# The first shift of the opening: half of its sum on VectorE for the latents, the context's part behind the first product

## Chip, core and metric

One NeuronCore of one Trainium2 chip runs the whole kernel. The metric is the device time of one execution in microseconds (us).

## The reference

One layer of a diffusion backbone over 1024 latent tokens with a prefix of 256 context tokens, width 1024, all in float32. Every sub-layer is normalised and then modulated by a shift, a scale and a gate, which are linear in SiLU of a conditioning vector: `c` for the latents, `c_ctx` for the context. The part that matters here, cut short:

```python
mod_lat = silu(c) @ w_mod + b_mod        # (1, 9 * 1024): nine pieces of 1024
mod_ctx = silu(c_ctx) @ w_mod + b_mod
ml, mc = split(mod_lat, 9), split(mod_ctx, 9)

def modulate(h, shift, scale):
    return h * (1.0 + scale) + shift

x  = x  + 0.5 * ml[2] * swiglu(modulate(rms_norm(x,  g1), ml[0], ml[1]), ffn1_w_in, ffn1_w_out)
cx = cx + 0.5 * mc[2] * swiglu(modulate(rms_norm(cx, g1), mc[0], mc[1]), ffn1_w_in, ffn1_w_out)
# then: short convolution and attention, merged; a second FFN; a final norm of x
```

So piece 0 of `w_mod` (1024 x 1024) gives the first shift, piece 1 the first scale, each for two vectors. The latents need them before the first matrix product of FFN 1 can start; the context needs them much later, since its tokens are read only after the latents' FFN is under way.

## The kernel before

Tokens lie along the free dimension, features along the 128 partitions. The latents come in two halves of 512 tokens, C0 and C1; the two-by-two blocks of each FFN product are formed by a Strassen-Winograd scheme with seven products (the class `Winograd`). A float32 operand is split into two parts (a rounded one and the rest), and each product is three matmuls: `split` takes a cast on ScalarE and a subtraction on VectorE or, where `lo_engines` says so, on GpSimd (POOL). Matrix tiles in the profile: `wl` and `wh` are split weights, `r` split left operands, `ps`, `pt`, `po` PSUM banks (five, two and one of them), `raw` a loaded weight, `rawm` a loaded tile of `w_mod`, `xtok` loaded tokens.

The program has one stretch at its beginning in which `strict[0]` is true: there every instruction of every engine, and every load in the queue of SyncE (SP), keeps the order in which the program writes it. After that a planner with costs of its own orders what is left free. The stretch in question, in the order written:

1. `fetch_tokens(C0)` loads four tiles of tokens, `fetch_mod(1, 0)` and `fetch_mod(0, 0)` load the first 512 columns of the scale and of the shift as four tiles of 512 KB each. Each tile holds two blocks of 128 rows of `w_mod`, so there are eight blocks, k = 0 to 7.
2. TensorE turns tokens. `mod10 = column_mod(1, 0, ...)` and `mod00 = column_mod(0, 0, ...)` make the first half of the scale and of the shift: for each k a matmul with the two columns of SiLU (latents and context) as the weights and the block (128 x 512) as the moving operand, all eight summed in one bank as two rows. The float32 product shows as two matmul records for each k. ScalarE copies the two rows (`mrow`), four small transposes turn them into columns, and `column_adds` on VectorE adds the bias into `modl` and `modc`. Both are generators; `run(g, n)` takes n steps of one.
3. `part_gain` makes the gain from the scale, and for each of four k `left_operand(0, k, mod11)` applies gain and shift to a tile of scaled tokens (VectorE for even k, ScalarE for odd) and splits it into `r`. Between the operands stand steps of `mod11 = second_mod(1, 1, ...)`: the other half of the scale for the latents alone, summed on VectorE in `macc` with one instruction for each k, the sum over the partitions by four matmuls against a column of ones (`summed_mod`). `part_gain` for the context stands behind the first operand.
4. `half1.start_together()` yields the first products of FFN 1 one by one: `run(start, 1)` first gives the two products for columns 0 and 1, each copied from its bank by ScalarE into `uc`, then one product a step. `half1.prefetch(n)` fills the list of loaded and split weights up to n.
5. Between these steps stand the rest of the opening: `scaled(k, pt)` (a copy of turned tokens by ScalarE, a scaling by VectorE), `turn` (the transposes of the tokens for the next two banks), the other half of the shift (`raws01`, `mod01`), the squares and transposes of the tokens of C1.

Of the kernel before, what the change touches and what calls it, by code (L numbers as in the profile page):

```python
# [9 lines left out]
F32 = mybir.dt.float32  # L10
# [3 lines left out]
ALU = mybir.AluOpType  # L14
# [4 lines left out]
P = 128  # L19
D = 1024  # L20
KD = D // P
# [28 lines left out]
def tile_dit_layer(  # L50
# [44 lines left out]
    act, dve, pool, pe, sp = (Engine(e) for e in (nc.scalar, nc.vector, nc.gpsimd, nc.tensor, nc.sync))  # L95

    const = ctx.enter_context(tc.tile_pool(name="const", bufs=1))
# [9 lines left out]
    def uniq(s):  # L107
        n_tiles[0] += 1
        return f"{s}_{n_tiles[0]}"
# [4 lines left out]
    def ttile(name, n=512, dt=F32):  # L114
        t = tpool.tile([P, 512], dt, tag="t", name=uniq(name))
        return t[:, :n]
# [4 lines left out]
    def ps_s(n=512):  # L121
        return psum.tile([P, 512], F32, tag="s", name=uniq("ps"), bufs=5)[:, :n]

    def ps_t(n=512):
        return psum.tile([P, 512], F32, tag="t", name=uniq("pt"), bufs=2)[:, :n]
# [4 lines left out]
    def matmul(out, w, x, start, stop, pinned=False, on=False):  # L130

        inst = pe.matmul(out, w, x, start=start, stop=stop, skip_group_check=on)
        if pinned:
            tc.keep_in_program_order(inst)

    def transpose(out, in_, pinned=False):
        n = in_.shape[0]
        inst = pe.transpose(out, in_, ident[:n, :n])
        if pinned:
            tc.keep_in_program_order(inst)  # L140
# [8 lines left out]
    make_identity(nc, ident[:])  # L149
    ones = const.tile([P, 1], F32, name="ones")  # L150
    dve.memset(ones[:], 1.0)
    ones_r = const.tile([P, 1], F32R, name="ones_r")
    act.copy(out=ones_r[:], in_=ones[:])

# [21 lines left out]
    def col(name, k=0):  # L176
        o = voff[name] + k
        return cols[:, o : o + 1]

    silu_c = const.tile([P, 16], F32, name="silu_c")  # L180
# [3 lines left out]
    modc = const.tile([P, 40], F32, name="modc")  # L184
# [113 lines left out]
    def summed_mod(m, half, acc):  # L298
        pm = ps_s(4)
        for j in range(4):  # L300
            matmul(pm[:, j : j + 1], acc[:, j * P : (j + 1) * P], ones[:], start=True, stop=True)
        column_adds(m, half, pm, (0,))

    def fetch_mod(m, half):
        raws = []
        for kk in range(KD // 2):
            raw = atile("rawm", (P, 2, 512))
            o = m * D + half * 512
            src = w_mod[0, kk * 256 : (kk + 1) * 256, o : o + 512].rearrange("(a p) n -> p a n", p=P)
            load(raw[:], src)  # L310
            raws.append(raw)
        return raws

    def column_adds(m, half, pm, streams):
        c0 = m * 8 + half * 4
        for i, v in enumerate(streams):
            dve.tensor_add(
                out=(modl, modc)[v][:, c0 : c0 + 4], in0=pm.rearrange("p (k v) -> p v k", v=len(streams))[:, i],
                in1=bcol[:, c0 : c0 + 4],
            )  # L320

    def column_mod(m, half, raws, bank):

        sc = silu_c[:].rearrange("p (v k) -> p k v", k=KD)
        pr = bank()
        for k in range(KD):
            matmul(pr[:2], sc[:, k], raws[k // 2][:, k % 2], start=(k == 0), stop=(k == KD - 1))
            if k % 2 and k < KD - 1:
                yield
        row = ttile("mrow")  # L330
        act.copy(out=row[:2], in_=pr[:2])
        yield
        pm = ps_t(8)
        for j in range(4):
            transpose(pm[:, 2 * j : 2 * j + 2], row[:2, j * P : (j + 1) * P])
        column_adds(m, half, pm, (0, 1))
        yield

    def second_mod(m, half, raws):

        acc = ttile("macc")
        for k in range(KD):
            raw, s = raws[k // 2][:, k % 2], silu_c[:, k : k + 1]
            if k:
                dve.scalar_tensor_tensor(out=acc, in0=raw, scalar=s, in1=acc, op0=ALU.mult, op1=ALU.add)
            else:
                dve.tensor_scalar(out=acc, in0=raw, scalar1=s, scalar2=None, op0=ALU.mult)
            yield
        yield
        summed_mod(m, half, acc)  # L350
        yield
        yield
# [9 lines left out]
    def part_gain(t, m, gname, s, a, b):  # L362
        mod, c0, o = (modl if s == "l" else modc), (m + 1) * 8, voff[gname]
        dve.tensor_scalar(
            out=t[:, a:b], in0=mod[:, c0 + a : c0 + b], scalar1=1.0, scalar2=math.sqrt(D), op0=ALU.add, op1=ALU.mult
        )
        dve.tensor_mul(out=t[:, a:b], in0=t[:, a:b], in1=cols[:, o + a : o + b])
# [70 lines left out]
    def run(steps, n=None):  # L438

        if n is None:  # L440
            for _ in steps:
                pass
        else:
            for _ in range(n):
                next(steps, None)
# [620 lines left out]
    def fetch_tokens(ch):  # L1066
        s, o, n = ch
        src = x[0] if s == "l" else ctxt[0]
        toks = []
        for j in range(n // P):  # L1070
            t = atile("xtok")
            load(t[:], src[o + j * P : o + (j + 1) * P, :])
            toks.append(t)
        return toks
# [17 lines left out]
    load_vectors("b", [("b", b_mod[0])])  # L1092
    t0 = fetch_tokens(C0)
    raws10, raws00 = fetch_mod(1, 0), fetch_mod(0, 0)
    mod10, mod00 = column_mod(1, 0, raws10, ps_t), column_mod(0, 0, raws00, ps_o)

    def column_pairs(w, offsets):
        return [tuple(w[:, o : o + P] for o in ab) for ab in offsets]
# [2 lines left out]
    gain1 = {s: const.tile([P, 8], F32, name=f"gain1_{s}") for s in "lc"}  # L1101
# [14 lines left out]
    def turn(toks, k, pt):  # L1116
        for j, t in enumerate(toks):
            transpose(pt[:, j * P : (j + 1) * P], t[:, k * P : (k + 1) * P])
# [10 lines left out]
    def left_operand(i, k, between=iter(())):  # L1129
        h, c = h0[k][:, i], k + 4 * i  # L1130
        if k % 2 == 0:
            dve.tensor_scalar(
                out=h, in0=h, scalar1=gain1["l"][:, c : c + 1], scalar2=modl[:, c : c + 1], op0=ALU.mult, op1=ALU.add
            )
        else:
            half1.shifted(h, c)
        run(between, 1 - k % 2)
        half1.keep(1 + i, k, h)
        run(between, 1 - k % 2)
# [6 lines left out]
    pr = ttile("pr")  # L1146
# [6 lines left out]
    run(mod10)  # L1153
    part_gain(gain1["l"], 0, "g1", "l", 0, 4)
    half1.prefetch(4, lo_engines=(pool, pool))
    run(mod00, 3)
    t1 = fetch_tokens(C1)
    raws11 = fetch_mod(1, 1)
    banks = {k: ps_s() for k in (4, 5)}
    for k, pt in banks.items():  # L1160
        turn(t0, k, pt)
    run(mod00)
    mod11 = second_mod(1, 1, raws11)
    for k in range(4):
        left_operand(0, k, mod11)
        if k == 0:
            part_gain(gain1["c"], 0, "g1", "c", 0, 4)
    start = half1.start_together()
    half1.prefetch(5, lo_engines=(pool, pool))
    for k, pt in banks.items():  # L1170
        scaled(k, pt)
    run(mod11, 2)
    run(start, 1)
    half1.prefetch(4, lo_engines=(pool, pool))
    banks = {k: ps_t() for k in (6, 7)}
    for k, pt in banks.items():
        turn(t0, k, pt)
        scaled(k, pt)
    raws01 = fetch_mod(0, 1)
    mod01 = second_mod(0, 1, raws01)  # L1180
    squares1 = token_squares(t1, ss1)
    run(mod11, 3)
# [120 lines left out]
    def context_rows(j):  # L1303

        raws = []
        for i in (j - 1, j):
            t = atile("raw")
            load(t[:], ffn1_w_out[0, i * P : (i + 1) * P, :])
            raws.append(t)
        return raws  # L1310
# [36 lines left out]
    for j in range(NH):  # L1347
        half1.side = side(j) if j >= SIDE_FROM else None
        if j > SIDE_FROM and j % 2:
            raws = context_rows(j)  # L1350
        u, c = half1.next_first()
        v, b = half1.second(u)
# [3 lines left out]
        if j == SIDE_FROM - 1:  # L1356
            for i in range(SIDE_FROM):
                if i % 2 == 0:
                    raws = context_rows(i + 1)
# [101 lines left out]
    for i in range(KD):  # L1461
# [6 lines left out]
        for ch, bg, gc in mixed():  # L1468
# [6 lines left out]
            for j in (0, 2):  # L1475
# [3 lines left out]
                    out=ya, in0=u[:, a + j - 1 : b + j - 1], scalar=col(f"w{j}", i), in1=ya, op0=ALU.mult, op1=ALU.add  # L1479
# [396 lines left out]
    for j in range(4):  # L1876
# [7 lines left out]
        out=gf[:], in0=cols[:, voff["gf"] : voff["gf"] + 8], scalar1=math.sqrt(D), scalar2=None, op0=ALU.mult  # L1884
# [96 lines left out]
    for j in range(NH):  # L1981
        if j > 1:
            run(late_steps, 3)
        u, c = fast.next_first()
        v, b = fast.second(u)
# [79 lines left out]
```

## Time and profile before

| | us |
|---|---|
| median of 3 runs (2669.16 to 2673.95) | 2670.07 |
| the profiled execution | 2671.16 |
| its span, first to last instruction | 2669.3 |
| TensorE matmuls, busy | 2628.8 |
| TensorE weight loads, busy | 2224.4 |
| VectorE busy | 2052.6 |
| ScalarE busy | 1192.0 |
| POOL busy | 548.8 |

The mean granted clock of TensorE was 0.996 of full speed. Rows of the timeline give the start, the duration, the engine, the line (nearly all have that of a helper, L88), the operation, the tile written and the tiles read, the shape, the count of merged instructions, and in brackets how long the engine was idle before and what ended that. PE is TensorE's matmul, PEld its weight load, DVE VectorE, ACT ScalarE, SPq the load queue of SyncE. In the table of stretches the columns are the stretch, its length, busy time and number of instructions for the engines, the granted clock, the busy share of the DMA engines and GB/s.

### The profile page before, as it was taken

The page shows a single profiled execution, that of the slowest core. Times are in us where ns is not written, and L with a number is a line of the kernel's source. Part 1 is how long each engine was busy: PE and PEld are TensorE (multiplying, and loading weights), DVE is VectorE, ACT ScalarE, POOL GpSimd, SP SyncE. Part 2 cuts the span into 40 slices and gives each one's busy share as a digit, 9 for nine tenths or more (in the row PEclk, how much of TensorE's full clock was granted, in tenths as well). Part 3 has the DMA queues.
Part 4 walks back from the last instruction along what each step waited for, and adds up shares of the span by engine and source line. Part 5 has one row for each costly group of instructions (what it writes and reads, how often), then busy time and mean ns, then how long its engine had stood idle before and what let it go on. Part 6 is the DMA issues. An engine that isn't in the chain of part 4 may idle for free. (4 is left out here: it accounts for less than half of the span.)

```text
span 2669.3 us, 37458 instructions
## 1 busy us (share of the span) xinstructions
PE 2628.8 (98%) x13557; PEld 2224.4 (83%) x13557; DVE 2052.6 (77%) x3412; ACT 1192.0 (45%) x2376; POOL 548.8 (21%) x425
## 2 busy tenths in 40 slices
PE   8999999999999999999999999999999999999998
PEld 5787998888888888888999888878788888888888
DVE  5988887875887899778687666786887787667975
ACT  5633443333454643333345666674346333334543
POOL 1244011211110044322033211000120444230200
PEclk9999999999999999999999999999999999999998
DMA  7655753335973444434413311003425654228731
GB/s 269 240 182 175 234 169 119 111 99 208 284 171 115 136 144 147 129 123 138 154 48 111 107 45 47 28 25 107 150 79 172 191 172 128 91 83 310 166 80 64
DMA packets 374769, 370.62 MB, mean 139 GB/s; under 512 B 28070, under 2 KB 264760, under 8 KB 374584
## 3 DMA queue, kind: packets, MB, share of 16 engines
q1 hardware_dynamic: 365560, 350.93, 39.9%
q0 software_dynamic: 9024, 17.30, 4.1%
q8 instruction: 106, 1.74, 0.3%
q14 instruction: 79, 0.65, 0.1%
HBM read 299.97 MB, written 68.16 MB: 138 GB/s over the span
## 5 line engine op out<-in xcount | busy, mean ns | idle before, releaser
L88 PE MATMUL ps<-r,wl 128*128 128x512 f32 x5496 | 1269.2, 391 | 15.5 <-DVE wl L88 7.7
L88 PEld LDWEIGHTS ps<-r,wl 128*128 128x128 f32 x5496 | 1028.2, 188 | 234.7 <-DVE wl L88 10.9
L88 ACT CAST wl<-s 128x512 fp32r<-128x512 f32 x266 | 164.1, 620 | 343.5 <-PE ps L88 259.1
L88 POOL TENSOR_TENSOR s<-raw 128x512 f32<-128x512 f32 x68 | 102.4, 1507 | 928.6 <-DMA raw<-in_ffn_w_in_dram 284.3
L88 ACT CAST wl<-raw 128x512 fp32r<-128x512 f32 x298 | 184.0, 620 | 206.4 <-PE ps L88 137.3
L88 DVE TENSOR_TENSOR wl<-raw,wl 128x512 fp32r<-128x512 f32 x296 | 209.4, 713 | 82.5 <-ACT wl L88 81.5
L88 DVE TENSOR_TENSOR wl<-s,wl 128x512 fp32r<-128x512 f32 x266 | 234.6, 883 | 29.9 <-ACT wl L88 28.3
L88 POOL TENSOR_TENSOR s<-raw,s 128x512 f32<-128x512 f32 x68 | 103.2, 1518 | 397.8 <-DVE wl L88 394.5
L88 DVE SCALAR_TENSOR_TENSOR macc<-rawm,silu_c,macc 128x512 f32<-128x512 f32 x168 | 146.4, 884 | 10.5 <-DMA rawm<-in_w_mod_dram 9.2
L88 PE MATMUL ps<-wh,r 128*128 128x256 f32 x768 | 142.2, 285 | 0.0
L88 DVE TENSOR_TENSOR u<-u,ps 128x512 f32<-128x512 f32 x171 | 116.1, 679 | 32.6 <-PE ps L88 31.9
L88 DVE TENSOR_TENSOR pts<-pt,pts 128x512 fp32r<-128x512 f32 x160 | 108.9, 687 | 39.3 <-ACT pts L88 38.0
L88 ACT CAST rh<-hid 128x512 fp32r<-128x512 f32 x132 | 81.5, 621 | 116.9 <-PE ps L88 100.4
L88 DVE TENSOR_REDUCE m<-ps 128x1 f32<-128x512 f32 (+1 forms) x192 | 111.0, 596 | 27.9 <-PE ps L88 27.0
L88 ACT CAST pts<-pt 128x512 fp32r<-128x512 f32 x160 | 93.0, 593 | 80.4 <-PE pt L88 80.0
L88 PE MATMUL ps<-rh,wl 128*128 128x512 f32 x360 | 122.1, 389 | 0.0
L88 PEld LDWEIGHTS ps<-wh,r 128*128 128x128 f32 x768 | 120.7, 192 | 0.2
L88 PE MATMUL po<-pts,vh 128*128 128x512 f32 x256 | 110.2, 437 | 0.8 <-ACT pts L88 0.7
L88 DVE TENSOR_TENSOR rl<-hid,rh 128x512 fp32r<-128x512 f32 x132 | 90.4, 687 | 26.7 <-ACT rh L88 12.3
L88 PE MATMUL ps<-wl,r 128*128 128x256 f32 x384 | 109.0, 284 | 0.0
L88 PE MATMUL ps<-kl,qs 128*128 128x512 f32 x384 | 105.9, 397 | 0.4 <-ACT pc L88 0.4
L88 POOL TENSOR_TENSOR s<-raw,raw 128x512 f32<-128x512 f32 x68 | 104.7, 1540 | 4.0 <-DVE macc L88 2.7
(300 smaller groups left out, 4892.7 us busy)
## 6 DMA issues: line engine op xcount, KB each, us to landing
raw<-in_ffn_w_in_dram SPq DMA_DIRECT2D x128, 512.0 KB
raw<-in_ffn_w_out_dram SPq DMA_DIRECT2D x72, 512.0 KB
rawm<-in_w_mod_dram SPq DMA_DIRECT2D x128, 256.0 KB
raw<-in_w_in_dram SPq DMA_DIRECT2D x61, 512.0 KB
hid<-hd SPq DMA_DIRECT2D x40, 512.0 KB
ws<-in_ffn_w_out_dram POOLq DMA_DIRECT2D x30, 512.0 KB, 6.5
ucd<-uc SPq DMA_DIRECT2D x26, 512.0 KB
hd<-c SPq DMA_DIRECT2D x39, 256.0 KB
```

The costliest lines, as they stand in the source:

```text
L88: inst = getattr(self.engine, name)(*args, **kw)
```

## The change

The generator of the first half of the shift is a new one, `shared_mod`. Of its eight blocks k = 0 to 3 stay matmuls with both columns of SiLU. The blocks k = 4 to 7 are summed on VectorE with the latents' values alone, and this sum is added into the same bank by one product whose weights are `first_row` (a column of ones for the latents' row, a column of zeros for the context's), so the latents' row is whole and the context's row holds half. Copy, transposes and `column_adds` are as before. Later the generator sums the blocks 4 to 7 on VectorE with the context's values, takes the sum over the partitions by four matmuls against `ones`, and adds it to `modc`.

In the order written, the VectorE adds for the latents take the place of the first two blocks (`run(mod00, 1)`), the matmuls of all four blocks stand behind the transposes of the scale, and the transposes of the next token banks stand between them and the product with `first_row`. The context's part and the context's `part_gain` stand behind `run(start, 1)`, the step with the first two products.

```diff
+    first_row = const.tile([P, 2], F32, name="first_row")
+    dve.memset(first_row[:, :1], 1.0)
+    dve.memset(first_row[:, 1:], 0.0)
...
+    def add_row(acc, raws, v, k, k0):
+        raw, s = raws[k // 2][:, k % 2], silu_c[:, v * 8 + k : v * 8 + k + 1]
+        if k > k0:
+            dve.scalar_tensor_tensor(out=acc, in0=raw, scalar=s, in1=acc, op0=ALU.mult, op1=ALU.add)
+        else:
+            dve.tensor_scalar(out=acc, in0=raw, scalar1=s, scalar2=None, op0=ALU.mult)
+
+    def shared_mod(m, half, raws, bank):
+
+        sc = silu_c[:].rearrange("p (v k) -> p k v", k=KD)
+        pr, acc = bank(), ttile("macc")
+        for k in range(4, KD):
+            add_row(acc, raws, 0, k, 4)
+        yield
+        for k in range(4):
+            matmul(pr[:2], sc[:, k], raws[k // 2][:, k % 2], start=(k == 0), stop=False)
+            if k % 2:
+                yield
+        matmul(pr[:2], first_row[:], acc, start=False, stop=True)
+        row = ttile("mrow")
+        act.copy(out=row[:2], in_=pr[:2])
+        yield
+        pm = ps_t(8)
+        for j in range(4):
+            transpose(pm[:, 2 * j : 2 * j + 2], row[:2, j * P : (j + 1) * P])
+        column_adds(m, half, pm, (0, 1))
+        yield
+        acc = ttile("macc")
+        for k in range(4, KD):
+            add_row(acc, raws, 1, k, 4)
+            yield
+        pm, c0 = ps_s(4), m * 8 + half * 4
+        for j in range(4):
+            matmul(pm[:, j : j + 1], acc[:, j * P : (j + 1) * P], ones[:], start=True, stop=True)
+        dve.tensor_add(out=modc[:, c0 : c0 + 4], in0=modc[:, c0 : c0 + 4], in1=pm)
+        yield
...
-    mod10, mod00 = column_mod(1, 0, raws10, ps_t), column_mod(0, 0, raws00, ps_o)
+    mod10, mod00 = column_mod(1, 0, raws10, ps_t), shared_mod(0, 0, raws00, ps_o)
...
-    run(mod00, 3)
+    run(mod00, 2)
     t1 = fetch_tokens(C1)
     raws11 = fetch_mod(1, 1)
     banks = {k: ps_s() for k in (4, 5)}
     for k, pt in banks.items():
         turn(t0, k, pt)
-    run(mod00)
+    run(mod00, 2)
     mod11 = second_mod(1, 1, raws11)
     for k in range(4):
         left_operand(0, k, mod11)
-        if k == 0:
-            part_gain(gain1["c"], 0, "g1", "c", 0, 4)
     start = half1.start_together()
     half1.prefetch(5, lo_engines=(pool, pool))
     for k, pt in banks.items():
         scaled(k, pt)
     run(mod11, 2)
     run(start, 1)
+    run(mod00)
+    part_gain(gain1["c"], 0, "g1", "c", 0, 4)
     half1.prefetch(4, lo_engines=(pool, pool))
```

`second_mod` now calls `add_row` for the same instructions as before.

More of the change, by code (lines that the diff above doesn't have):

```diff
@@ L342, in second_mod @@
         for k in range(KD):
[L343 to L347, printed above, removed]
+            add_row(acc, raws, 0, k, 0)
             yield
```

## The prediction

> **What bounds the kernel now.** I read the page first, then the timeline of the first 48 us on all engines, then the table of stretches (busy time, granted clock, DMA) over the same time, and last TensorE's waits up to 272 us.
>
> ```profile
> span 2669.3 us, 37458 instructions
> PE 2628.8 (98%) x13557; PEld 2224.4 (83%) x13557; DVE 2052.6 (77%) x3412; ACT 1192.0 (45%) x2376; POOL 548.8 (21%) x425
> ```
>
> TensorE is busy for 98% of the span, so time that it loses anywhere is lost unless it stood idle later for something else. Busy TensorE is not useful TensorE, though: the question for an edit in the opening is how far the matmuls behind it move.
>
> ```profile
> 21.06 0.57 ACT L88 COPY mrow<-pt 2x512 f32<-2x512 f32 x1 [7.24 <-PE pt L88]
> 22.37 1.45 DVE L88 TENSOR_TENSOR wl<-raw,wl 128x512 fp32r<-128x512 f32 x2 [3.26 <-ACT wl L88]
> 22.67 0.41 PE L88 MATMUL pt<-ident,mrow 2*128 2x2 f32 x4
> 23.01 5.31 PE L88 MATMUL po<-rawm,silu_c 128*2 128x512 f32 x12
> 28.25 1.09 PE L88 MATMUL ps<-ident,xtok 128*128 128x128 f32 x8
> 28.36 0.58 ACT L88 COPY mrow<-po 2x512 f32<-2x512 f32 x1 [3.73 <-PE po L88]
> 29.27 0.41 PE L88 MATMUL pt<-ident,mrow 2*128 2x2 f32 x4
> 31.17 0.50 PE L88 MATMUL ps<-r,wl 128*128 128x512 f32 x1 [1.49 <-ACT r L88]
> ...
> 38.51 1.02 PEld L88 LDWEIGHTS pt<-ident,xtok 128*128 128x128 f32 x8
> 39.50 2.60 PEld L88 LDWEIGHTS ps<-r,wl 128*128 128x128 f32 x12
> 43.35 0.97 PEld L88 LDWEIGHTS ps<-ones,macc 128*128 128x128 f32 x8 [0.19 <-DVE macc L88]
> 44.24 2.59 PEld L88 LDWEIGHTS ps<-r,wl 128*128 128x128 f32 x12
> ```
>
> The reader sees one chain. The product of the shift, 16 matmuls into po, ends with the 12 of 23.01; the eight transposes of the tokens follow at 28.25, ScalarE copies the two rows at 28.36, TensorE turns them at 29.27, VectorE adds the bias, and the first matmul of FFN 1 starts at 31.17. From 38.51 on TensorE is never free: transposes, twelve matmuls of the next product at 39.50, and so on. TensorE also takes its work strictly as written here: the transposes of 38.51 read tokens and banks that were there long before, and yet stand behind the whole first product. That the sums at 43.35 waited 0.19 us for VectorE's accumulator, with the twelve matmuls of 44.24 queued behind them, says the same.
>
> ```profile
> 30.38 0.48 DVE L88 TENSOR_SCALAR macc<-rawm,silu_c 128x512 f32<-128x512 f32 x1
> 31.15 0.69 DVE L88 TENSOR_TENSOR r<-h,r 128x512 fp32r<-128x512 f32 x1 [0.29 <-ACT r L88]
> 32.42 0.16 DVE L88 TENSOR_SCALAR gain_c<-modc 128x4 f32<-128x4 f32 x1
> 32.70 0.69 DVE L88 TENSOR_TENSOR r<-h,r 128x512 fp32r<-128x512 f32 x1
> ...
> 38.10 1.53 DVE L88 SCALAR_TENSOR_TENSOR macc<-rawm,silu_c,macc 128x512 f32<-128x512 f32 x2
> 43.22 0.48 DVE L88 TENSOR_SCALAR macc<-rawm,silu_c 128x512 f32<-128x512 f32 x1
> 43.73 1.54 DVE L88 SCALAR_TENSOR_TENSOR macc<-rawm,silu_c,macc 128x512 f32<-128x512 f32 x2
> ```
>
> VectorE is the second tight engine of this stretch. From 31.15 on it makes the four left operands (r), with steps of the other sum (macc) and the context's gain between them; then it scales two banks and does two more macc steps, ending at 38.10 + 1.53 = 39.63.
>
> **The change, part by part.**
>
> (1) Four of the eight rows of the first shift go from TensorE to VectorE, latents only. Twelve matmuls took 5.31 us, so about 0.43 us each to the next one's start; the product drops from 16 to 8 and gains 2 for the accumulator's sum: 6 fewer, 2.6 us. Not all of it reaches the chain. The turn of the other half's row (22.67 now) no longer stands behind four of these matmuls and waits for ScalarE's copy instead (to 21.06 + 0.57 = 21.63): TensorE is idle until about 21.7, turns until 22.05 (23.01 - 22.67 = 0.34), does 8 matmuls until 25.5, then the eight transposes (29.27 - 28.25 = 1.02) until 26.5, then the 2 until 27.4, plus 0.15 to the end of the last. The copy of 0.58 now starts after the transposes, not beside them, and ends near 28.2. So the turn comes at 28.25 in place of 29.27: 1.0 us earlier.
>
> (2) VectorE's four adds for it cost as one start of 0.48 (to the next: 43.73 - 43.22 = 0.51) and three of 1.54 / 2 = 0.77: 2.8 us. They go into the 3.26 us in which VectorE stood idle ahead of the weight subtraction at 22.37, so I cost them at nothing: if their last rows land late and push that subtraction and the first gain by half a microsecond, these are still needed only past 28 us. Two small memsets at the start: nothing. The waits of SP's and POOL's queues are not moved by this part.
>
> (3) The 1.0 us does not all arrive, because the next thing on VectorE reads a transfer.
>
> ```profile
> 20.00:31.00 11.00, 9.68 (x35) 2.86 (x33) 3.92 (x10) 4.13 (x7) 2.48 (x2) 1.00 1.07 398
> 23.25 1.36 ACT L88 CAST wl<-raw 128x512 fp32r<-128x512 f32 x2 [0.16 <-DMA raw<-in_ffn_w_in_dram]
> ```
>
> The macc start of 30.38 reads the first tile of w_mod for another piece. Ahead of it in SP's queue stand 16 tiles of 0.524 MB (two token groups, two pieces of w_mod), four of 0.262 MB, and itself: 9.96 MB. The third of the 0.262 MB tiles, with which 7.08 MB are through, was waited for by ScalarE until 23.2 (the cast of 23.25), and the stretch moved 398 GB/s, its DMA engines full. So that tile lands near 23.2 + (9.96 - 7.08) / 0.398 = 30.4, an estimate, just when it is read now. Bounds for the operands: moved by the full 1.0, or only by what follows from the reader at 30.3 (its end 30.8 against the subtraction of 31.15: 0.35). To either comes 32.70 - 32.42 = 0.28 us, the context's gain, which moves out. I take 0.6 us earlier, near the transfer's end because the count fits it (ends 1.3 and 0.5).
>
> (4) The context part. Behind the first product, in program order, stand four more VectorE adds (2.8 us, as in 2), eight matmul records against ones, an addition, and the moved gain. VectorE reaches them only after the macc steps that end at 39.63, so it starts at 39.63 - 0.6 = 39.03 and ends at 41.8. TensorE ends its first product near 38.5, sooner rather than later, and its next instructions are now the sums over this accumulator. It waits. Behind them queue the transposes of 38.51, the scalings, the loads' releases and the product of 39.50, on all engines.
>
> (5) The adds meet a POOL instruction.
>
> ```profile
> 38.25 1.27 ACT L88 COPY uc<-ps 128x512 f32<-128x512 f32 x2 [0.90 <-PE ps L88]
> 39.42 0.62 ACT L88 CAST wh<-raw 128x512 fp32r<-128x512 f32 x1
> 40.12 1.30 POOL L88 TENSOR_TENSOR wh<-raw,wh 128x512 fp32r<-128x512 f32 x1 [2.37 <-ACT wh L88]
> ...
> 392.88 1.30 POOL L88 TENSOR_TENSOR s<-raw 128x512 f32<-128x512 f32 x1 [4.00 <-DMA raw<-in_ffn_w_in_dram]
> 392.94 1.78 DVE L88 SCALAR_TENSOR_TENSOR macc<-rawm,silu_c,macc 128x512 f32<-128x512 f32 x1
> ```
>
> POOL's subtraction of 40.12 follows ScalarE's two copies of the first product's result and a cast; those come as early as before or up to 0.6 us earlier, so POOL runs at about 39.6 to 41.4, inside the new adds. At 392.94 the same kind of add began with such a POOL instruction and took 1.78 instead of 0.74 to 0.77: 1.0 us. Bounds: 0 if they miss each other, 1.3 if a whole POOL instruction is waited for; I take 1.1. The Trainium skill ("SBUF — State Buffer", Who interferes with whom) says that a VectorE instruction with two SBUF inputs and a GpSimd instruction that reads SBUF exclude each other for a whole instruction; these adds have two such inputs. By that rule the term would be 1.3 and the sum 0.2 larger; the pair of rows agrees with it.
>
> So the accumulator is ready at 41.8 + 1.1 = 42.9, TensorE has stood still for about 4.4 us, the sums take 44.24 - 43.35 = 0.89, the transposes 39.50 - 38.51 = 0.99, and the second product starts at 44.8 instead of 39.50: 5.3 us late. The 0.19 wait at 43.35 goes, since VectorE is no longer the later one there. Together +5.1 (ends: with 1.3 and no meeting +3.3, with 0.5 and a whole one +5.4).
>
> (6) The clock.
>
> ```profile
> 30.00:32.00 2.00, 0.61 (x2) 0.29 (x2) 1.71 (x4) 1.47 (x3) 0.00 (x0) 0.92 1.05 409
> 32.00:34.00 2.00, 2.00 (x5) 1.61 (x6) 1.97 (x6) 0.61 (x2) 0.00 (x0) 0.50 1.08 376
> 34.00:36.00 2.00, 2.00 (x7) 1.54 (x7) 1.96 (x4) 1.97 (x4) 0.00 (x0) 0.73 1.10 392
> ...
> 266.46 0.73 PE L88 MATMUL ps<-r,wl 128*128 128x512 f32 x2 [2.13 <-ACT wl L88]
> 268.00:269.00 1.00, 1.00 (x3) 0.50 0.03 10
> ```
>
> After a pause of 1.49 us at 31.17, with only transposes ahead of it, the granted clock was 0.50 for about 3.4 us (0.92, 0.50 and 0.73 over three stretches of 2 us); after one of 2.13 us at 266.46 it was 0.50 too. A pause of 4.4 us should do the same. Half clock for 3.4 us costs at most 1.7 us, and less where it begins inside the pause: between 0 and 1.7, I take 1.1, nearer the upper end since both rows drop after work resumed. The Trainium skill ("TensorE: Matmul & The Clock Gate", HAM oscillation — how this bites in real kernels) puts the limit at gaps above some 3.4 us; this trace drops after shorter ones, so the measurement decides. By the page the drop would hang on the POOL meeting, and without it the sum would lose this term.
>
> (7) What follows. Is it given back?
>
> ```profile
> 59.23 0.59 ACT L88 COPY uc<-ps 128x512 f32<-128x512 f32 x1 [1.59 <-PE ps L88]
> 60.36 0.69 DVE L88 TENSOR_TENSOR wl<-raw,wl 128x512 fp32r<-128x512 f32 x1 [0.85 <-ACT wl L88]
> 97.32 6.19 PE L88 MATMUL ps<-r,wl 128*128 128x512 f32 x26 [1.16 <-ACT uc L88]
> 105.18 4.39 PE L88 MATMUL ps<-r,wl 128*128 128x512 f32 x18 [1.66 <-DVE wl L88]
> ```
>
> TensorE's next idle times are 1.16 at 97.32 and 1.66 at 105.18, 2.8 us. They would absorb if what TensorE waits for there kept its time. But VectorE's row at 60.36 waited for a cast that stood behind ScalarE's copy of 59.23, which waited 1.59 us for TensorE: the work starts in step with TensorE and moves with it. I take 0 back (ends -2.8 and 0). The extra bank and two accumulators are costed at nothing: the eight banks are free in time; if a slot were short, the load behind it would wait, which no row shows.
>
> Sum: +5.1 + 1.1 + 0 = +6.2 us. The profiled execution took 2671.16 us (span 2669.3 and 1.9 around it) and would take 2677.4. It lies 1.1 above the median of the three runs, so the median goes from 2670.07 to **2676.3**, 0.23% slower.
>
> **The rivals.** *No meeting with POOL*, or a half clock that falls wholly into the pause: each leaves +5.1, 2675.2, just under 0.2%. For it: both are questions of half a microsecond. Against: the predicted times overlap.
>
> *Given back*: the waits at 97.32 and 105.18 swallow 2.8 us, +3.4, 2673.5. Against it the coupling in (7).
>
> *The other side: TensorE does not stand at the sums.* If VectorE ended the context's adds before the first product's end, or TensorE took them behind the second product, only the earlier start (-0.6) and the 0.89 us of sums would remain: +0.3, 2670.4, no slower than a measurement can tell. It decides at 38.5 us: VectorE would have to be 3.3 us faster without POOL, 4.4 with it. The order at 38.51 and 43.35 speaks against.
>
> *Another order later.* The rest of the program is arranged by a planner from its own costs; a changed beginning may shift it by some microseconds either way, which no row prices. TensorE's whole idle time is 2669.3 - 2628.8 = 40 us.
>
> **How the numbers follow.** The forecast (waiting, meeting, one stretch of half clock, carried to the end) 0.50; its own range 2674.8 to 2677.8, from (3), (5) and (6). The two cases at 2675.2 together 0.28; given back 0.12; no standing still 0.06; another order 0.04, half each way. A measurement of this kernel tells about 0.2%, 5.3 us. Slower by more: 0.42 of the forecast's 0.50, 0.13 of the 0.28 and 0.02: 0.57. Within: the rest of these, given back and no standing still, less 0.02: 0.39. Faster: 0.04. The range 2672.0 to 2678.8 takes in given back and two stretches of half clock, and leaves out the other side.
>
> **What would show it.** The turn near 28.25 and the first FFN matmul 0.3 to 1 us before 31.17 show (1) and (3). A wait of TensorE of 3 to 5 us "DVE macc" ahead of the matmuls on ones near 42 to 43 us shows (4); one add of 1.5 us or more there shows (5); clock near 0.5 between 41 and 47 shows (6); the idle times near 100 and 108, again 1.2 and 1.7, show (7). I am wrong if TensorE runs on from its first product without a pause, or if these late waits shrink.

## The result and the profile after

The changed kernel took 2681.11 us (median of 6 runs, 2679.58 to 2684.75), the kernel before 2671.14 (6 runs on the same chip): ratio 1.0043, 95% interval 1.0033 to 1.0053, so 10.0 us slower. The forecast was 6.2 us slower, 2676.3; the direction was right, the size was not. The profiled execution took 2679.73 us, 8.6 above the one before.

Totals from the page of the changed kernel:

```profile
span 2677.9 us, 37475 instructions
PE 2629.5 (98%) x13559; PEld 2224.9 (83%) x13559; DVE 2054.8 (77%) x3423; ACT 1189.8 (44%) x2376; POOL 546.3 (20%) x425
```

TensorE's busy time grew by 0.7 us and the span by 8.6: nearly all of the loss is standing still. The timeline of the changed kernel on the same stretch shows where (VectorE, TensorE and POOL; other rows left out):

```profile
27.91 0.41 PE L88 MATMUL pt<-ident,mrow 2*128 2x2 f32 x4 [0.67 <-ACT mrow L88]
...
29.80 0.50 PE L88 MATMUL ps<-r,wl 128*128 128x512 f32 x1 [1.49 <-ACT r L88]
31.38 0.49 DVE L88 TENSOR_SCALAR macc<-rawm,silu_c 128x512 f32<-128x512 f32 x1 [2.28 <-DMA rawm<-in_w_mod_dram]
31.78 0.69 DVE L88 TENSOR_TENSOR r<-h,r 128x512 fp32r<-128x512 f32 x1
...
32.52 8.07 PE L88 MATMUL ps<-r,wl 128*128 128x512 f32 x23 [2.22 <-DVE r L88]
...
38.73 1.53 DVE L88 SCALAR_TENSOR_TENSOR macc<-rawm,silu_c,macc 128x512 f32<-128x512 f32 x2
40.17 0.48 DVE L88 TENSOR_SCALAR macc<-rawm,silu_c 128x512 f32<-128x512 f32 x1
40.69 3.21 DVE L88 SCALAR_TENSOR_TENSOR macc<-rawm,silu_c,macc 128x512 f32<-128x512 f32 x3
41.81 1.54 POOL L88 TENSOR_TENSOR wh<-raw,wh 128x512 fp32r<-128x512 f32 x1 [3.44 <-ACT wh L88]
43.95 1.14 PE L88 MATMUL ps<-ones,macc 128*128 128x1 f32 x8 [3.36 <-DVE macc L88]
44.95 1.95 PE L88 MATMUL pt<-ident,xtok 128*128 128x128 f32 x8
...
46.55 2.63 PE L88 MATMUL ps<-r,wl 128*128 128x512 f32 x7
```

The chain up to the first matmul of FFN 1 is shorter, as meant: the turn of the second row comes at 27.91 instead of 29.27, the first matmul at 29.80 instead of 31.17. Then the lead is lost at once. VectorE's macc start, which stands ahead of the first subtraction (31.78), stood idle for 2.28 us until its row of `w_mod` had landed and began at 31.38, 1.0 us later than before (30.38), so TensorE waited 2.22 us after its first matmul. The context's adds run from 40.17 to 43.90, TensorE waits 3.36 us for them ("DVE macc"), and the second product starts at 46.55 instead of 39.50: 7.0 us late. Matching matmuls of the two traces lie 7.6 us apart from 46 to 94 us. From there to 1934 us they stay between 7.3 and 8.8 us apart, except near 100 us (up to 10.3) and 275 us (6.3): new waits and windows of half clock lie in other places there (near 106 us in the changed kernel, near 267 us in the kernel before).

The late landing has its own row. In the table of stretches (granted clock, DMA share and GB/s are the last three columns) the changed kernel from 20 to 31 us:

```profile
20.00:31.00 11.00, 7.49 (x29) 2.37 (x27) 6.25 (x13) 5.46 (x9) 2.48 (x2) 1.00 1.07 366
```

Before it was 398 GB/s, with the DMA engines as full (1.07). The order of the loads in SP's queue is that of before. The clock around the wait, changed kernel:

```profile
42.00:44.00 2.00, 0.05 (x1) 0.05 (x1) 1.86 (x2) 0.00 (x0) 1.35 (x1) 1.00 1.16 300
44.00:46.00 2.00, 2.00 (x13) 2.00 (x14) 0.40 (x3) 0.00 (x0) 0.00 (x0) 0.70 1.08 275
46.00:48.00 2.00, 2.00 (x9) 1.71 (x8) 1.14 (x2) 1.17 (x2) 0.00 (x0) 0.50 0.54 144
48.00:50.00 2.00, 2.00 (x10) 1.66 (x9) 1.97 (x4) 0.00 (x0) 0.00 (x0) 0.95 0.01 3
```

### The profile page after: what moved, and what is told of

The parts are those of the page before. It is cut to its first block, busy times and chain, and to the rows that moved or that the text cites. A ratio compares the mean times of both kernels' runs of the same rounds, so it can differ in the third digit from the quotient of the medians.

```text
span 2677.9 us, 37475 instructions
## 1 busy us (share of the span) xinstructions
PE 2629.5 (98%) x13559; PEld 2224.9 (83%) x13559; DVE 2054.8 (77%) x3423; ACT 1189.8 (44%) x2376; POOL 546.3 (20%) x425
```

## The experiments

The theory at this point: the pause at the context's sums and the half clock behind it are the loss. The rival: the added work costs the same wherever it lies. Four kernels, measured beside a kernel before of 2669.87 us (median of 11 runs).

### 1. The context part later

`run(mod00)` and the context's gain leave their place behind the first step; the adds go into VectorE's idle time ahead of the third of the products made one by one, the sums one step later.

```diff
     run(mod01, 3)
+    run(mod00, 4)
     run(start, 1)
...
     turned((4, 5))
+    run(mod00)
+    part_gain(gain1["c"], 0, "g1", "c", 0, 4)
```

> The first shift shared with VectorE as in the change, but the context's four adds stand later, in VectorE's idle stretch ahead of the third lone product, and its sums on TensorE one step behind that. Theory (the cost is TensorE standing still at the context's sums, behind VectorE's adds): no wait of TensorE near 40 us, second product within 1 us of its old start (39.5), total within 4 us of the kernel before (2667 to 2675). Rival A (the first half, read early on VectorE, delays the operands): the second product starts 1 to 2 us late and the total stays 2 to 5 us above. Rival B (later half-clock stretches make the difference): still 4 us or more above.

Measured: 2681.7 us, ratio 1.0045 (1.0032 to 1.0059). No better, as rival B had it, although the wait of 3.4 us was gone and matmuls lay only 2.4 to 3.9 us behind those of the kernel before for most of the trace up to 1934 us. The profiled execution took 2672.15, the shortest of five, so its trace doesn't show what the median paid.

### 2. No context part

```diff
     run(start, 1)
-    run(mod00)
     part_gain(gain1["c"], 0, "g1", "c", 0, 4)
```

> The change without its context part: the context's shift lacks the rows of four blocks. What is left is the first half on VectorE and the moved gain. Theory: 0 to 1.5 us faster than before at the second product (38.0 to 39.5), total -2 to +1 us. Rival A: operands late as in the changed kernel (+0.6 us at the third operand), no gain or 1 to 2 us slower.

Measured: 2676.47 us, 1.0027 (1.0016 to 1.0038). Without the context's work there is no wait at its sums, and the kernel was still 6.6 us slower than before, with less to do: slower than both the theory and the rival had it. In its trace the second product starts at 39.47 us, as early as before (39.53), and matching matmuls fall behind only from 95 us on (3.1 us at 108). So the pause is not the whole.

### 3. The pause alone

The kernel before with the context's four adds and sums repeated behind the first product, into a column that nothing reads.

```diff
     run(start, 1)
+    context_again(0, 0, raws00)   # 4 adds of blocks 4 to 7, 4 matmuls on ones, 1 addition
     half1.prefetch(4, lo_engines=(pool, pool))
```

> The kernel before, with the full first product of the shift kept on TensorE, and the context's four adds and four sums done once more behind the first product, into a column that nothing reads. Theory: the wait at the sums (3 to 4 us), one add slowed by POOL (about 0.9 us) and the cold clock behind it come back without the first half of the change: second product at 45 to 47 us, total +6 to +9 us. Rival A: less than half of the loss (under 4 us).

Measured: 2679.64 us, 1.0035 (1.0022 to 1.0047). From its timeline:

```profile
40.82 3.21 DVE L88 SCALAR_TENSOR_TENSOR macc<-rawm,silu_c,macc 128x512 f32<-128x512 f32 x3
41.00 1.69 POOL L88 TENSOR_TENSOR wh<-raw,wh 128x512 fp32r<-128x512 f32 x1 [2.49 <-ACT wh L88]
...
44.08 1.87 PE L88 MATMUL ps<-ones,macc 128*128 128x1 f32 x8 [4.30 <-DVE macc L88]
```

A wait of 4.30 us where the prediction had put 4.4, beside a POOL instruction as it had said, and 9.8 us in all, a little over the 6 to 9 expected. So the context's added part by itself, without the new tile and without the shorter first product, can cost what the whole change costs.

### 4. The sums one product later

The adds stay behind the first product, the sums go behind the second.

```diff
     run(start, 1)
-    run(mod00)
-    part_gain(gain1["c"], 0, "g1", "c", 0, 4)
+    run(mod00, 4)
...
     run(mod11, 3)
     run(start, 1)
+    run(mod00)
+    part_gain(gain1["c"], 0, "g1", "c", 0, 4)
     run(squares1, 1)
```

> The changed kernel with the context's VectorE adds where they were, but its sums on TensorE one product later. Theory (the place in TensorE's order is what costs, not the load of VectorE): second product back near 39.5 to 41, the wait shifted to the later sums and shorter, 0 to 2 us; total +1 to +3.5 us. Rival (VectorE's 2.8 us and the meeting with POOL cost wherever they stand): total +6 us or more.

Measured: 2677.99 us, 1.0032 (1.0019 to 1.0045). TensorE's wait at the sums fell to 0.53 us and matmuls were 2.7 us behind from 44 to 90 us, yet the kernel is still 8.1 us slower than before, which is the rival's time. Kernels 1, 2 and 4 have one thing in common with the changed one. Their stretches from 20 to 31 us, first that of kernel 1:

```profile
20.00:31.00 11.00, 8.05 (x30) 2.46 (x28) 6.09 (x13) 4.92 (x8) 2.49 (x2) 1.00 1.08 366
```

The same stretch of kernel 2:

```profile
20.00:31.00 11.00, 7.38 (x29) 2.37 (x27) 5.88 (x13) 5.56 (x9) 2.49 (x2) 1.00 1.08 367
```

And of kernel 4:

```profile
20.00:31.00 11.00, 7.12 (x28) 2.37 (x27) 5.93 (x13) 5.58 (x9) 2.49 (x2) 1.00 1.08 367
```

Kernel 3, which has the pause but not the new tile, moved as much as the kernel before:

```profile
20.00:31.00 11.00, 10.44 (x37) 2.95 (x34) 4.26 (x9) 3.43 (x6) 2.48 (x2) 1.00 1.07 398
```

What the slow ones share is `first_row`. It is allocated among the constants, which lie ahead of all other tiles, in steps of 32 bytes per partition. In the compiled programs every tile of 2 KB or more starts at 256 modulo 512 bytes in the kernel before and in kernel 3, and at 288 modulo 512 in the changed kernel and in 1, 2 and 4. The second theory: that shift of 32 bytes slows every load.

### 5. The tile alone

```diff
     dve.memset(ones[:], 1.0)
+    first_row = const.tile([P, 2], F32, name="first_row")
+    dve.memset(first_row[:, :1], 1.0)
+    dve.memset(first_row[:, 1:], 0.0)
```

> The kernel before with nothing added but the tile of the first row and its two memsets; nothing reads it. Tiles are laid out in steps of 32 bytes per partition, so this tile moves every tile of 2 KB or more from a start at a multiple of 256 bytes (256 modulo 512) to 32 bytes behind one. Address theory: every load's packets are slower with that start; from 20 to 30 us the rows should show 364 to 366 GB/s where the kernel before shows 397, the row of the third product's weights should land about 1 us later, VectorE's first step of the next shift moves from 30.4 to about 31.4, and the time is 2 to 5 us above the kernel before (2672 to 2675 beside 2670). Rival, that the slower loads come from the changed work of the opening (other engines' traffic, other order of loads): 397 GB/s, and the time within 0.1% of before.

Measured, beside a kernel before of 2670.8 us (32 runs, as for 6 to 8): 2675.49 us, 1.0019 (1.0010 to 1.0028). The stretch in this kernel:

```profile
20.00:31.00 11.00, 9.51 (x35) 2.87 (x32) 3.75 (x10) 4.68 (x8) 2.48 (x2) 1.00 1.08 367
```

And TensorE's timeline in it at 97 us:

```profile
97.09 0.33 PE L88 MATMUL pt<-ident,xtok 128*128 128x128 f32 x1 [0.46 <-DMA xtok<-in_ctx_dram]
...
98.43 0.33 PE L88 MATMUL pt<-ident,xtok 128*128 128x128 f32 x1 [0.80 <-DMA xtok<-in_ctx_dram]
```

A tile that nothing reads takes the loads from 398 to 367 GB/s and costs 4.7 us. The row for the next shift landed at 30.86 us (kernel 8 on the same chip: 29.22). TensorE is 1.4 us behind from 37 to 90 us, and at 97 us it waits for the context's tokens (0.46 and 0.80), for which the trace of before shows no wait.

### 6. The change without the shift of addresses

```diff
-    ones = const.tile([P, 1], F32, name="ones")
-    dve.memset(ones[:], 1.0)
     first_row = const.tile([P, 2], F32, name="first_row")
     dve.memset(first_row[:, :1], 1.0)
     dve.memset(first_row[:, 1:], 0.0)
+    ones = first_row[:, :1]
```

> The changed kernel with the column of ones taken as the first column of the first row's tile, so that no tile is added and all addresses are those of the kernel before; every instruction of the change stays. Address theory: 397 GB/s from 20 to 30 us again, macc starts at 30.4 instead of 31.4, the first three operands come 0.5 us before those of the kernel before, TensorE still waits 3 to 4 us at the context's sums, and the second product starts 5 to 6.5 us late; time 2675 to 2678 (+5 to +8), 3 to 6 below the changed kernel. Rival (addresses do not matter): 365 GB/s, macc at 31.4, time 2679.6 to 2682.

Measured: 2678.17 us, 1.0030 (1.0020 to 1.0039). The stretch in this kernel:

```profile
20.00:31.00 11.00, 7.33 (x28) 2.87 (x29) 6.51 (x15) 5.42 (x9) 2.52 (x2) 0.96 1.06 400
```

And its timeline:

```profile
29.35 0.49 DVE L88 TENSOR_SCALAR macc<-rawm,silu_c 128x512 f32<-128x512 f32 x1 [1.11 <-DMA rawm<-in_w_mod_dram]
...
41.65 1.86 PE L88 MATMUL ps<-first_row,macc 128*128 128x1 f32 x8 [4.24 <-DVE macc L88]
43.37 1.95 PE L88 MATMUL pt<-ident,xtok 128*128 128x128 f32 x8
44.97 3.37 PE L88 MATMUL ps<-r,wl 128*128 128x512 f32 x9
```

The loads are back and the pause is left: 7.4 us slower than before, the forecast being 6.2. This kernel keeps both memsets, so the slow loads come from where the tile lies and not from filling it. The second product starts at 44.97, where the prediction had 44.8, but that is partly luck. The accumulator was ready at 41.6 instead of 42.9, because the row of the next shift landed a microsecond earlier than estimated, and half clock stretched the sums and transposes to 3.3 us (41.65 to 44.97) where the prediction had 1.9 and put the clock behind them.

### 7. The late context part without the shift

Kernel 1 with the tile of kernel 6.

> The kernel of the late context part (context's adds in VectorE's idle time ahead of the third lone product, its sums a step later), with the tile of ones shared as in the kernel with restored addresses. Address theory and the stall at the sums together: neither loss is left, 397 GB/s, no wait of over 1 us for macc at the context's sums; TensorE's first matmul is 1 us and the operands 0.5 us earlier than before, so 2668 to 2671 (-2 to +1). Rival, that moving the context's part behind the first product costs the time wherever it lies (a wait of another kind each time): 2674 to 2680.

Measured: 2673.97 us, 1.0010 (1.0001 to 1.0019). Against kernel 1 (1.0045) this is the clearest price of the addresses: the two intervals don't overlap. It is also 4.2 us below kernel 6, the price of the pause. It missed its expectation (2668 to 2671) by 3 us, and its timeline shows a shorter wait left at the sums:

```profile
52.48 1.05 PE L88 MATMUL ps<-first_row,macc 128*128 128x1 f32 x8 [0.83 <-DVE macc L88]
```

### 8. A shift of 256 bytes, and 12. of 128

```diff
     dve.memset(ones[:], 1.0)
+    pad = const.tile([P, 64], F32, name="pad")   # 12: [P, 32]
+    dve.memset(pad[:, :2], 0.0)
```

> The kernel before with an unused tile of 256 bytes per partition beside the ones: all tiles of 2 KB or more move from 256 modulo 512 to multiples of 512 bytes. If a start at a multiple of 256 bytes is all that counts, 397 GB/s from 20 to 30 us and a time within 0.1% of before (2668 to 2672). If the unit is 512 bytes or more, the loads are faster than before (over 400 GB/s from 20 to 30 us) and the time falls by 1 to 4 us. If any displacement costs, it is slower like the kernel with the tile of the first row alone.

> The kernel before with an unused tile of 128 bytes per partition beside the ones: tiles of 2 KB or more start 128 bytes behind a multiple of 256. If the loads need starts at multiples of 256 bytes, 364 to 370 GB/s from 20 to 30 us, as with 32 bytes; if 64 or 128 bytes are enough, 395 to 402 GB/s, as with 256.

Measured: with 256 bytes 2672.1 us, 1.0002 (0.9993 to 1.0011), no difference; with 128 one run of 2672.39, which can't tell a time. The stretch of kernel 8:

```profile
20.00:31.00 11.00, 9.51 (x35) 2.97 (x33) 4.98 (x11) 4.20 (x8) 2.54 (x2) 1.00 1.06 401
```

And of kernel 12:

```profile
20.00:31.00 11.00, 9.91 (x35) 2.86 (x33) 3.74 (x10) 3.82 (x7) 2.48 (x2) 1.00 1.09 367
```

128 bytes slow the loads as much as 32 do; 256 don't. The median packet of 2 KB between 20 and 35 us took 84 ns in the kernel before and in 6 and 8, 87 to 88 in the changed kernel, in 5 and in 12. The Trainium skill ("DMA: Bandwidth & Descriptors", How a descriptor splits into AXI transactions) says that a descriptor is split into transactions of 256 bytes, that a transaction must start at a multiple of 256, and that for a descriptor which starts elsewhere the bytes before its start are fetched too and cost beats. The page tells this of what a transaction reads; here the destination of a load was moved, so it bears on this case only by likeness. The direction agrees, and so does the unit. The size doesn't follow from it: an estimate by that page's beats of 32 bytes gives 65 beats instead of 64 for a packet of 2 KB moved by 32 bytes, and 68 for 128 bytes, while these runs show the same 8% of the rate for both.

### 9. Work in the pause

Kernel 6 with four matmuls that wait for nothing late between the first product and the context's sums; the sums overwrite their result.

```diff
-    pm, c0 = ps_s(4), m * 8 + half * 4
+    bank, c0 = ps_s(), m * 8 + half * 4
+    pm = bank[:, :4]
+    for _ in range(4):
+        matmul(bank, ident[:], raws[2][:, 0], start=True, stop=True)
```

> The changed kernel with restored addresses, and four matmuls of 128x512 (identity by the first latent tile of the context's rows, into the bank of the sums, whose result the sums overwrite) put between the first product and the context's sums, where TensorE waited 4.24 us at macc: some 3.8 us of work that depends on nothing late. The sums start no later than without them. Clock theory: the granted clock of 0.5 from 40.4 to 47.2 us comes from the pause; without the pause the sums take about 1.05 instead of 1.86 us, the transposes about 1.2 instead of 1.95, the second product starts at 42.6 to 43.6 instead of 45.0, and the time is 2 to 4 us below the kernel with restored addresses (2674 to 2676 beside 2678). Rival (the low clock is the pattern of the opening and has nothing to do with the pause): the window stays and the time is within 1 us of it, or above.

Measured, beside a kernel before of 2671.04 us (29 runs, as for 10 to 12): 2677.12 us, 1.0024 (1.0015 to 1.0033), against 1.0030 for kernel 6. Timeline of kernel 9:

```profile
37.61 3.60 PE L88 MATMUL ps<-rawm,ident 128*128 128x512 f32 x8
41.81 1.05 PE L88 MATMUL ps<-first_row,macc 128*128 128x1 f32 x8 [0.60 <-DVE macc L88]
42.73 1.07 PE L88 MATMUL pt<-ident,xtok 128*128 128x128 f32 x8
43.55 3.00 PE L88 MATMUL ps<-r,wl 128*128 128x512 f32 x12
```

The table of stretches has two of these us in kernel 6:

```profile
44.00:46.00 2.00, 2.00 (x10) 1.81 (x9) 0.71 (x2) 1.17 (x2) 0.00 (x0) 0.50 0.13 38
```

and in kernel 9:

```profile
44.00:46.00 2.00, 2.00 (x11) 1.63 (x10) 1.95 (x4) 0.47 (x1) 0.00 (x0) 1.00 0.14 41
```

The sums don't start sooner (41.81 against 41.65) and what follows still gets faster: sums 1.05 instead of 1.86, transposes 1.07 instead of 1.95, second product at 43.55 instead of 44.97. From 44 us on, matching matmuls lie 3.8 us behind those of the kernel before, instead of 6.3. So the half clock behind the pause is the pause's doing in these two traces and cost 2.5 us there. The total doesn't show that much: 6.1 us above the kernel before instead of 7.4, over the 2674 to 2676 expected, and the two intervals overlap.

### 10 and 11. The next shift's steps behind the operands

Kernel 10 is kernel 7 with this edit and the context's sums one more product later; kernel 11 is the kernel before with this edit alone.

```diff
     for k in range(4):
-        left_operand(0, k, mod11)
+        left_operand(0, k)
...
-    run(mod11, 2)
+    run(mod11, 6)
```

> The kernel of the late context part with restored addresses, with two more moves: the first four steps of the next shift go behind the four operands on VectorE (they wait for a load's landing and stand ahead of the subtractions that the first product needs), and the context's sums go one product later still. If the first product is held by VectorE's wait for the row of the next shift (1.41 us at macc before the subtraction of 29.73), TensorE's wait of 1.35 us at its second matmul shrinks to under 0.7, the product runs 2 to 2.5 us ahead of the kernel before, the 0.8 us wait at the sums of 52.5 goes, and the time is 2666 to 2670. Rival: what is won in the opening is given back at the next load or clock window, and the time stays within 1.5 us of the kernel of the late context part (2672.5 to 2675.5).

> The kernel before, with the first four steps of the next shift moved behind the four operands on VectorE and nothing else. There the row had landed before the first subtraction was ready, so the steps cost only their own 0.48 and 0.75 us on VectorE ahead of a subtraction: 0.2 to 0.8 us earlier for the first product, 2669.5 to 2671 beside 2670.8, which is no difference that can be told. If the interleaved steps do bound the four operands, 2667 to 2669.

Measured: kernel 10 2677.04 us, 1.0020 (1.0011 to 1.0028); kernel 11 2674.76, 1.0011 (1.0002 to 1.0020). Both missed on the slow side. Kernel 13 below is kernel 10 without this edit. Timeline of kernel 10:

```profile
31.04 6.04 PE L88 MATMUL ps<-r,wl 128*128 128x512 f32 x23 [0.22 <-DVE r L88]
...
37.58 4.91 DVE L88 SCALAR_TENSOR_TENSOR macc<-rawm,silu_c,macc 128x512 f32<-128x512 f32 x5
...
42.41 1.28 DVE L88 TENSOR_TENSOR h<-pt,pr 128x512 f32<-128x512 f32 x2
...
43.15 1.05 PE L88 MATMUL pt<-ident,xtok 128*128 128x128 f32 x4 [1.99 <-DVE h L88]
```

And one row of its stretches:

```profile
42.00:54.00 12.00, 9.42 (x33) 7.75 (x34) 10.74 (x18) 3.11 (x7) 1.27 (x1) 0.57 0.18 55
```

The first product does run early (its wait after the first matmul is 0.22, and the transposes behind it start at 36.91 instead of 38.74). But the six steps now stand together ahead of the scaling that frees a bank (42.41), TensorE waits 1.99 us for it and 1.43 more at the next sums, and for 12 us its clock is 0.57 on average. A lead of 1.8 us at 42 us became a delay of 6.0 at 50. Kernel 11 has the same two waits without any part of the change:

```profile
43.12 0.66 PE L88 MATMUL pt<-ident,xtok 128*128 128x128 f32 x4 [0.88 <-DVE h L88]
46.04 1.87 PE L88 MATMUL ps<-ones,macc 128*128 128x1 f32 x8 [2.27 <-DVE macc L88]
```

Between the operands the steps had filled VectorE's waits for ScalarE's casts, and cost little there: without them VectorE stands idle for 0.69 and 0.68 us ahead of the subtractions at 33.55 and 34.92 of kernel 11.

### 13 and 14. Neither loss

Kernel 13 is kernel 7 with the context's sums one more product later. Kernel 14 also spreads the steps: two behind the second operand, three behind the scaling, and the next shift's sums one product later.

```diff
-        left_operand(0, k, mod11)
+        left_operand(0, k, mod11 if k == 2 else iter(()))   # 14
...
-    run(mod11, 2)
+    run(mod11, 3)                                           # 14
...
     turned((6, 7))
+    run(mod00)                                              # 13 and 14
+    part_gain(gain1["c"], 0, "g1", "c", 0, 4)
```

> The kernel of the late context part with restored addresses, its context sums one more product later and nothing else. There TensorE waited 0.83 us at those sums and the shift against the kernel before went from -0.3 to +1.9 us at that place. If that wait is the whole of what the change still costs, the shift stays at -0.3 to +0.5 there and the time is 2669.5 to 2672 beside 2671; if the context's adds cost the time in another place (a later wait, a load of the context's tokens that starts later), 2673 to 2675 as before this edit.

> As the kernel with the context's sums one more product later, and the next shift's first two steps behind the second operand instead of the first (they wait for the landing ahead of the first subtractions), one more step behind the scaling of the turned tokens, and the next shift's sums one product later. If the pauses at 30 us and at the sums both bind, the first product runs 1.5 to 2 us ahead of the kernel before, no pause of over 0.6 us follows until 90 us, and the time is 2667.5 to 2670. Rival, after the run that put six steps in one place: steps moved on VectorE hold the next bank's release or the next sums, a pause of 1 us or more comes back at 40 to 55 us, and the time is 2672 to 2678.

Measured, beside 2669.13 us (21 runs): kernel 13 2672.31, 1.0006 (0.9996 to 1.0016); kernel 14 2670.6, 1.0004 (0.9996 to 1.0013). No difference from the kernel before can be told for either. Their medians are 3.2 and 1.5 us above its, so both missed what was expected of them, level for kernel 13 and a gain for kernel 14. The waits of TensorE in kernel 14 from 28 to 92 us:

```profile
PE ps L88 <- ACT r L88: 1.5, 1, 1.5
PE pt L88 <- ACT mrow L88: 0.7, 1, 0.7
PE ps L88 <- DVE macc L88: 0.4, 1, 0.4
PE ps L88 <- DVE r L88: 0.2, 1, 0.2
```

With the addresses restored and no pause of over 1.5 us left, the change costs nothing that these runs can tell; the intervals leave room for up to 0.16%, some 4 us. It wins nothing either: matmuls of kernel 14 run 1.2 to 2.4 us ahead from 33 to 54 us and are level at 56; the context's added sums and their wait (0.4) lie between. No version here beat the kernel before.

## Why the prediction was wrong, point by point

(1) Right: the turn came 1.36 us earlier where 1.0 was forecast, the first matmul 1.37. The extra 0.4 is no more than traces with the same opening differ: in kernel 8, which only pads, the first matmul of FFN 1 starts at 30.81 instead of 31.17.

(2) The step that failed. "Two small memsets at the start: nothing. The waits of SP's and POOL's queues are not moved by this part." The instructions cost nothing, but the tile that they fill moved every large tile behind it by 32 bytes, and took the loads from 398 to 366 GB/s. The tile alone costs 4.7 us (kernel 5). With everything of the change but the moved addresses, the kernel is 7.4 us slower (kernel 6): 1.2 over the forecast's 6.2 and inside the range, which reaches from 1.9 to 8.7 above the kernel before. With them it is 10.0, above it. The four adds themselves were hidden, as forecast.

(3) The mechanism was right, the size off for the same reason. The row was put at 30.4; it landed at 31.36, and the first subtraction came 0.63 us late (31.78 against 31.15) instead of 0.6 early. So the context's adds on VectorE began 1.1 us later than forecast (40.17 against 39.03). The landing also differs from trace to trace. VectorE's read that waits for it began between 30.80 and 31.38 in the six traces with moved addresses, and between 29.32 and 29.51 in kernels 6, 7, 9 and 13, whose addresses are those of before. So with the old addresses the estimate of 30.4 would have been too late for those traces.

(4) and (5) Right. TensorE stood at the sums. The three later adds took 3.21 us, 1.07 each beside a POOL instruction against 0.77 alone: 0.9 against the 1.1 forecast. The wait was 3.36 us and not 4.4, because the first product itself ended later: after the longer wait at 32.52 the half clock of the opening lasted 6.8 us instead of 3.4.

(6) Right in kind. The clock fell just after TensorE resumed (0.70, 0.50, 0.95 over three stretches of 2 us), which is a loss of 0.6 + 1.0 + 0.1 = 1.7 us: the upper end of the range, where 1.1 was taken. In kernel 6 the half clock lasts twice as long, and by kernel 9 it costs 2.5 us there, more than the forecast's upper end. Of the 1.4 us between the 6.2 forecast and the 7.6 that the traces show up to 94 us, 1.0 is the accumulator, ready at 43.90 instead of 42.9; the rest goes with the clock.

(7) Right in the sum, not in the way. The changed kernel at the place of the two late waits:

```profile
104.12 0.33 PE L88 MATMUL pt<-ident,xtok 128*128 128x128 f32 x1 [0.85 <-DMA xtok<-in_ctx_dram]
...
106.00 12.19 PE L88 MATMUL ps<-r,wl 128*128 128x512 f32 x44 [1.33 <-ACT uc L88]
```

The wait for ScalarE's copy stayed (1.33 us, 1.16 before). The second one, 1.66 us at 105.18 before, is gone: the 44 matmuls run through. So one of the two waits did shrink, which the prediction had named as a sign against it. A new wait of 0.85 us for the context's tokens, a load, and a window of half clock near 106 us took more than that: the two traces are 7.6 us apart at 94 us and 8.6 at 108.

The rest is beyond 1934 us. In the profiled execution a further half-clock window near 1942 us added 2, later waits 1.6, and another order of the last 30 us took 2.6 off. That the median lost 10.0 and the profiled execution 8.6 can't be split further with these runs. Nor do the parts add up: the tile alone 4.7, the change without it 7.4, both together 10.0; the intervals of the last two (1.0020 to 1.0039 and 1.0033 to 1.0053) overlap, so what the tile costs inside the changed kernel is not measured by itself. What is shown is that without the two losses the change can't be told from the kernel before (kernels 13 and 14), and that with either alone it is slower. Not settled is why kernel 1 lost 11.8 us with the shift of addresses and kernel 7 only 3.2 without, more than the tile's own price; the wide interval of kernel 1's five runs leaves room for chance.

## What to carry to other kernels

A small constant isn't free if it is allocated ahead of the buffers that the loads fill: compare the start addresses of these buffers modulo 256 before and after an edit, and let the constant share an existing tile, as kernel 6 does, or its padding. Compare GB/s of a load-bound stretch first, ahead of any explanation by the moved work. And price a pause of the matrix engine with the half clock behind it; where a wait can't be avoided, matmuls that depend on nothing late can keep the clock (kernel 9, whose total gained no more than the noise), and steps that fill another engine's idle time are not cheaper gathered in one place.

## What the runs showed of the hardware

A start of the destination 32 or 128 bytes off a multiple of 256 took the loads of the opening (20 to 31 us) from 398 to 401 GB/s down to 366 or 367, with the DMA engines equally busy; 256 bytes more changed nothing. All 16 traces fall into these two groups by their addresses: ten without such an offset, six with it. For the clock, two short pauses did what the prediction had expected of one long one: 1.99 and 1.43 us within 3 us of each other gave 0.57 over 12 us (kernel 10). Single pauses of 0.60 (kernel 9) and 0.83 us (kernel 7) left it at full speed, and so did the 1.66 us at 105.18 in the kernel before, while the 1.49 us near 30 us were followed by half clock in all these traces but one, that of kernel 10 (1.00 from 28 to 42 us). So the length alone doesn't decide it, and what else does stays open. Up to 2600 us the low windows of these traces last 3.4 us, or two or three times that.
